# GLA and HGRN over blocks of 512 tokens with all states before all outputs, and dense groups of 24 matmuls that are not broken

## The chip, the cores and the metric

The kernel runs on one core of one Trainium2 chip. The metric is the device time of one execution in microseconds (us); the time before is the median of three runs, 3616.11 us (3611.39 to 3624.22).

The engines are named as in the profile: PE is TensorE's matmuls and PEld its weight loads, DVE is VectorE, ACT ScalarE, POOL GpSimd, SP SyncE, which issues the DMAs.

## What is computed

A decoder of two layers (`DEPTH`), each with four recurrent mixers side by side and a cross attention, for one prompt of 2048 tokens and for eight samples of eight tokens that start from stored states. All four mixers read one projection of the normalized input and write into one output projection:

```python
proj = h @ P['w_in'][l]
p_ret, p_hgrn, p_gla, p_rwkv = jnp.split(proj, ...)
# ret, HGRN, GLA: a gated linear recurrence per token and head
S_t = diag(exp g_t) S_{t-1} + k_t v_t^T ;  o_t = S_t^T q_t
# RWKV-7
S_t = S_{t-1} diag(w_t) - (S_{t-1} kk_t)(kk_t*a_t)^T + v_t k_t^T ;  o_t = S_t r_t
out = jnp.concatenate([o_ret, o_hgrn, o_gla, o_rwkv], axis=-1) @ P['w_out'][l]
x = x + out
x = x + cross_attend(rmsnorm(x, P['norm_x'][l]), ...)
```

HGRN and ret have four heads of 64 keys, GLA four heads of 32 keys, all with 64 values per head. In ret the decay g is one constant per head, in GLA and HGRN it differs from token to token and key to key. The outputs are normalized per head and multiplied by a silu gate.

## The kernel before

**Blocks.** The prompt is worked off in four blocks of 512 tokens (`TB`, NB = 4) in either layer. `block()` emits one block: RWKV's projections and RWKV itself, then GLA's projections and GLA, HGRN's, ret's, the gates and the output projection. Within a block each mixer runs in two halves of 256 tokens (`Seg(False)`, nt = 2 tiles of 128 tokens). Block 0 of a layer also makes the samples' projections, and the sample mixers are put into block 0 (RWKV, GLA) and block 1 (HGRN, ret) by the table `TURN`.

**Dense and small products.** The projections are dense: a panel of 128 output columns takes 24 matmuls of 128x128 weights (three products of high and low parts for each of 8 slices of the input), into the PSUM pool `psd`. The recurrences are small products, of 32 to 128 rows. RWKV, ret and the samples take their PSUM tiles from `psa` and `psc` in turn (lane "ac"), GLA and HGRN from `psb` (lane "b").

**Who sets the order.** The order of each engine is fixed when the program is built, by a list scheduler that takes the ready instruction of highest priority, so that dense matmuls fall into the waits of the small chains. `held()` (lines 212 to 217) decides where a run of matmuls may be broken: every `run[0]`-th matmul of a run has its own priority, and the others are raised by `HOLD` so that they follow at once. `run[0]` is `DENSE` = 12 for a panel of the projections, `SMALL` = 48 for the small products; the output projection sets a run of 12 of its own accord with `DENSE` as well.

**GLA and HGRN.** `dyadic()` computes the scores within a tile of 128 tokens in seven levels s = 1, 2, 4 to 64 (`LEVELS`): at each level a set of 64x32 products (`psb<-dn_hq,dn_hf`), a masked copy into the scores `sT` on DVE (line 736), then the decays are multiplied into q and k (`q_step`, `k_step`; DVE) and into the running totals `tot` (POOL). In GLA two heads of 32 keys share 64 rows; `apart()` makes two masked copies of q by multiplying it with `hm32` on DVE. `outputs()` then goes from tile to tile: it reads the state S for tile t, adds the scores times v, and updates S before tile t + 1. `head_norm()` normalizes `osb`, the outputs; ret's `osb` lies in the tile of `rqT`.

**Memory.** RWKV, ret and the samples' mixers have scratch pools that begin at the lower end of SBUF's free part (`left`: wk1, wk1s, wk4 and others), GLA and HGRN at the upper end (`right`: wk2, wk3). A pool's tiles wait one by one for the earlier tiles that lay at the same place. `wrp` holds three buffers (tag "w") for raw weights, which are staged in block 0 only; the later blocks load weights that are already split.

Of the kernel before, what the change touches and what calls it, by code (L numbers as in the profile page):

```python
# [43 lines left out]
DENSE = 12  # L44
# [89 lines left out]
def decoder(ctx, tc, I, C, O):  # L134
# [428 lines left out]
    class Seg:  # L563
        def __init__(self, sample):
            self.sample = sample
            self.P = SN if sample else 128
            self.nt = 1 if sample else 2
            self.n = self.P * self.nt
            self.levels = SLEVELS if sample else LEVELS
# [26 lines left out]
    def outputs(seg, sT, at, v, qd, S, NG, NC, kT, tot, wp, eps, center, evac, state_out=None):  # L596


        P, nt = seg.P, seg.nt
        KD = 128 // NG  # L600
        NP = NG // 2
        if not seg.sample:
            po = PS("r").rearrange("p (t n) -> p t n", t=2)
            p5 = po.rearrange("p t (c g j d) -> p t c g j d", c=NC, g=2, j=NP)
            es = [slice(0, 64), slice(64, 128)]
            for t in range(nt):
                for c in range(NC):
                    for j in range(NP):
                        for e in es:
                            mm(p5[e, t, c, :, j, :], qd[:, c, j, t * 128 + e.start:t * 128 + e.stop], S[:, c, :], True, False)  # L610
                        for g in range(2):
                            h = c * NG + g * NP + j
                            x = sT[:, at(t, h)].rearrange("p e n -> p (e n)")
                            for e in es:
                                mm(po[e, t, h * 64:(h + 1) * 64], x[:, e], v[:, t, h * 64:(h + 1) * 64], False, True)
                pu = PS("r")[:, :NC * 64].rearrange("p (c n) -> p c n", c=NC)
                for h in range(NH):
                    c, g = divmod(h, NG)
                    mm(pu[g * KD:(g + 1) * KD, c, :], kT[:, t, h * KD:(h + 1) * KD], v[:, t, h * 64:(h + 1) * 64])
                for c in range(NC):  # L620
                    for p in range(2):
                        gs = slice(64 * p, 64 * p + 64)
                        blk = S[gs, c, p * 64:(p + 1) * 64]
                        V.scalar_tensor_tensor(blk, blk, tot(t, c)[gs], pu[gs, c, :], ALU.mult, ALU.add)
            tags = ("rqT", "rkT", None) if center else ("qx2", "qx2", 2)
            o = wp.tile([128, 2, 256], F32, name="osb", tag=tags[0], bufs=tags[2])
            A.activation(o, po, AF.Copy)
            head_norm(o, 128, 2, eps, center, wp, tags[1:], evac)
            return
        bm = sample_const("bmask", wp)  # L630
        pa = PS("r")
# [27 lines left out]
    def place(NG, NC, nt):  # L659

        NP = NG // 2

        def at(t, h):
            c, g = divmod(h, NG)
            p, j = divmod(g, NP)
            return ((p * nt + t) * NC + c) * NP + j
        return at

    def dyadic(seg, q, k, a, NG, NC, sT, wp):
# [10 lines left out]
        mine = lambda x, p: x[:, p * w:(p + 1) * w]  # L680

        def apart(i):
            if NP == 1:
                return q.unsqueeze(2)
# [6 lines left out]
        def products(s, f):  # L691
# [10 lines left out]
            for p in range(2):  # L702
                yield (mine(sT[:P], p)[:, :, 0, :].rearrange("p u (b f s) -> p u b f s", f=2, s=s)[:, :, :, f, :],
# [7 lines left out]
        def q_step(s, tot, x):  # L711
# [5 lines left out]
            new = wp.tile([128, NC, n // (2 * s)], F32, name=f"tot{s}", tag=f"tot{s}")  # L717
# [9 lines left out]
        tt(V, q, q, a, ALU.mult)  # L727
        tot = q_step(1, a, q.unsqueeze(2))
        Q[0] = apart(1)
        for li, s in enumerate(seg.levels):  # L730
# [6 lines left out]
            else:  # L737
                A.activation(sT[64:128, :, 1, :], sT[64:128, :, 0, :], AF.Copy)
                G.memset(sT[64:128, :, 0, :], 0.0)
                ps = [PS("r")[:, :NC * NP * 64].rearrange("p (c g n) -> p c g n", c=NC, g=NP) for _ in range(2)]  # L740
                for c in range(NC):
                    for t in range(nt):
                        for p in range(2):
                            mm(ps[p][64 * t:64 * t + 64, c], k[rows[p], c, t * P:t * P + 64], Q[0][rows[p], c, :, t * P + 64:t * P + 128])
                for t in range(nt):
                    for p in range(2):
                        o = mine(sT[0:64], p)[:, t * NC * NP:(t + 1) * NC * NP, 1, :]
                        A.activation(o, ps[p][64 * t:64 * t + 64].rearrange("p c g n -> p (c g) n"), AF.Copy)
# [4 lines left out]
        return Q[0], tot  # L753
# [18 lines left out]
    def gain(on, col):  # L772
        def f(ps):
            A.activation(on, ps, AF.Copy, scale=col)
        return f

    def plain(on):
        def f(ps):
            A.activation(on, ps, AF.Copy)
        return f  # L780

    def R_gla(l, seg, st, d, on, wp):
        c = cols[l]
        n = seg.n
        qk, v, sm = d["qk"], d["v"], d["sm"]
# [12 lines left out]
        sT = wp.tile([128, seg.nt * NH, seg.P // 64, 64], F32, name="sT", tag="sT")  # L798
        qd, tot = dyadic(seg, qk[:, 0:1, :], qk[:, 1:2, :], a, 4, 1, sT, wp)
        at = place(4, 1, seg.nt)  # L800
        kT = totok(qk[:, 1:2, :], 1, seg, wp, "gmn", 128)
        if seg.sample:
# [4 lines left out]
            outputs(seg, sT, at, v, qk[:, 0:1, :], S, 4, 1, kT, decay, wp, 32 * RMS_EPS, False,  # L807
                    gain(on, c["gla_norm"][:, 0:1]), lambda: sample_state_out(S, O[7][l], 32))
        else:
            outputs(seg, sT, at, v, qd, st, 4, 1, kT, lambda t, cc: tot[:, cc, t:t + 1], wp, 32 * RMS_EPS, False,  # L810
                    gain(on, c["gla_norm"][:, 0:1]))

    def R_hgrn(l, seg, st, d, on, wp):
# [8 lines left out]
        sT = wp.tile([128, seg.nt * NH, seg.P // 64, 64], F32, name="sT", tag="sT")  # L822
        qd, tot = dyadic(seg, q, f, a, 2, 2, sT, wp)
        at = place(2, 2, seg.nt)
        kT = totok(f, 2, seg, wp, "ha", 256)
        if seg.sample:
# [4 lines left out]
            outputs(seg, sT, at, v, q, S, 2, 2, kT, decay, wp, 4 * RMS_EPS, False,  # L831
                    gain(on, c["hgrn_norm"][:, 0:1]), lambda: sample_state_out(S, O[5][l], 64))
        else:
            outputs(seg, sT, at, v, qd, st, 2, 2, kT, lambda t, cc: tot[:, cc, t:t + 1], wp, 4 * RMS_EPS, False,
                    gain(on, c["hgrn_norm"][:, 0:1]))

    def R_ret(l, seg, st, d, on, wp):
# [23 lines left out]
        at = lambda t, h: t * NH + h  # L861
# [12 lines left out]
        if seg.sample:  # L874
# [397 lines left out]
    def block(l, b, act, hts, st, smp, on, ons, ds, op):  # L1272
# [4 lines left out]
        pr, sa = Seg(False), Seg(True)  # L1277
        carry = st["carry"]
# [102 lines left out]
        for hb in range(2):  # L1381
            with within("wk2", hb, 2), on_lane("b"), right("wk2") as wp:
                R_gla(l, pr, st["gla"], dict(qk=h2(qk, hb), v=t2(gv, hb), sm=sm[:, hb * 256:(hb + 1) * 256]), h2(on["gla"], hb), wp)
        if smp:
            ds["gla"] = dict(qk=qks, v=gvs, sm=sms)
# [38 lines left out]
        for hb in range(2):  # L1424
            with within("wk3", hb, 2), on_lane("b"), right("wk3") as wp:
                R_hgrn(l, pr, st["hgrn"], dict(q=h2(hq, hb), f=h2(hf, hb), v=t2(hv, hb)), h2(on["hgrn"], hb), wp)
# [595 lines left out]
```

## Time and profile before

| what | value |
|---|---|
| median of 3 runs | 3616.11 us |
| the profiled execution's own time | 3606.43 us |
| its span | 3604.6 us |
| mean granted clock of TensorE | 0.968 |
| PE busy | 3366.3 us, 93% |
| PEld busy | 2835.7 us, 79% |
| DVE busy | 2112.9 us, 59% |
| ACT busy | 1274.3 us, 35% |
| POOL busy | 553.0 us, 15% |

Busy time of PE is a sum of modelled lengths of pipelined matmuls, so a busy PE may still be short of its peak; that is why starts are compared below, from one row to the next, and not lengths. A clock of 1.00 stands for 2.4 GHz; the other level is 1.2 GHz. An "idle before" in brackets names the engine and the tile that came last before the instruction could start.

### The profile page before, as it was taken

What the parts mean: (1) busy time and instruction counts of PE and PEld (TensorE: products, weight loads), DVE (VectorE), ACT (ScalarE), POOL (GpSimd) and SP (SyncE); (2) the same over time, 40 slices, a digit from 0 to 9 for tenths busy, and PEclk for the clock granted to TensorE, in tenths of its full rate; (3) what the DMA queues carried; (4) which work ended last, traced back from release to release, by engine and by line L of the source; (5) the groups of instructions that cost most, each with busy time, mean ns of one, the idle gap of its engine ahead of it and who ended that gap; (6) DMA issues with size and microseconds to landing.
All of it is one profiled execution on the core that took longest, in us unless ns stands there. A gap on an engine that the chain in (4) does not pass through costs nothing.

```text
span 3604.6 us, 85661 instructions
## 1 busy us (share of the span) xinstructions
PE 3366.3 (93%) x36138; PEld 2835.7 (79%) x36138; DVE 2112.9 (59%) x6047; ACT 1274.3 (35%) x2729; POOL 553.0 (15%) x680
## 2 busy tenths in 40 slices
PE   7998799998999999999999997999889999999998
PEld 5877688886978888888877866878678888878887
DVE  5677545675436754576446765467644567446754
ACT  4442334422243324332344332443213333244323
POOL 3323231020000100011122242111100011000100
PEclk9999899998999999999999997999989999999999
DMA  6522565235662254324453255542445522542255
GB/s 191 184 98 89 180 218 192 77 112 163 200 215 90 82 196 150 135 76 173 170 172 121 83 155 175 197 153 94 136 153 186 176 98 92 188 160 103 76 195 188
DMA packets 241957, 530.79 MB, mean 147 GB/s; under 512 B 66854, under 2 KB 179750, under 8 KB 197542
## 3 DMA queue, kind: packets, MB, share of 16 engines
q1 hardware_dynamic: 241574, 525.31, 42.5%
q8 instruction: 285, 4.67, 0.5%
q14 instruction: 98, 0.80, 0.1%
HBM read 410.10 MB, written 115.16 MB: 146 GB/s over the span
## 4 chain that ended last, share of the span: by engine, by line
PE 75%; DVE 12%; ACT 5%; issue 3%; DMA 3%; POOL 2%; SPq 0%; POOLq 0%; ACTq 0%; DVEq 0%
PE psd L221 39%; PE psc L221 13%; PE psa L221 11%; PE psb L221 6%; PE psa L263 2%; PE psb L263 2%; PE psc L263 2%; DVE rsq L227 1%; DMA wraw<-in_w_in 1%; POOL whl L227 1%; DVE osb L227 1%; DVE hri L283 1%; DVE hss L552 1%; DVE dn_hq L227 0%; DMA whl<-w_low 0%
## 5 line engine op out<-in xcount | busy, mean ns | idle before, releaser
L221 PE MATMUL psd<-act,whl 128*128 128x512 f32 (+1 forms) x4032 | 1008.5, 402 | 28.6 <-DVE th L1266 12.8
L221 PEld LDWEIGHTS psd<-act,whl 128*128 128x128 f32 (+1 forms) x4032 | 741.4, 189 | 203.5 <-DVE th L1266 15.3
L221 PE MATMUL psd<-whl,act 128*128 128x256 f32 x3840 | 541.4, 292 | 7.0 <-POOL whl L227 3.3
L221 PEld LDWEIGHTS psd<-whl,act 128*128 128x128 f32 x3840 | 482.9, 193 | 28.6 <-issue 9.2
L227 POOL TENSOR_TENSOR whl<-wraw,whl 128x1024 fp32r<-128x1024 f32 (+1 forms) x90 | 218.0, 2428 | 383.3 <-ACT whl L349 366.2
L271 POOL TENSOR_TENSOR ri<-ri,mhalf 128x1 f32<-128x1 f32 (+1 forms) x87 | 50.6, 582 | 1103.9 <-DVE ri L270 1065.3
L221 PE MATMUL psd<-whl,oh 128*128 128x256 f32 x1152 | 211.4, 284 | 0.0
L221 PEld LDWEIGHTS psd<-whl,oh 128*128 128x128 f32 x1152 | 177.4, 189 | 0.9 <-issue 0.3
L221 PE MATMUL psd<-whl,ol 128*128 128x256 f32 x576 | 162.8, 283 | 0.0
L349 ACT ACTIVATE whl<-wraw 128x1024 fp32r<-128x1024 f32 (+1 forms) x90 | 94.0, 1048 | 120.9 <-DMA wraw<-in_w_in 40.5
L932 ACT ACTIVATE Xb<-X 32x256 f32<-32x256 f32 (+1 forms) x164 | 67.6, 412 | 166.0 <-DVE X L951 119.9
L221 PEld LDWEIGHTS psd<-whl,ol 128*128 128x128 f32 x576 | 108.5, 188 | 1.0 <-DVE ol L227 1.0
L736 DVE COPY_PREDICATED sT<-upack,psb 128x128 f32<-128x128 uint8 x320 | 89.6, 327 | 33.2 <-PE psb L221 31.5
L227 DVE TENSOR_TENSOR x<-x,psd 128x256 f32<-128x256 f32 x72 | 30.3, 421 | 132.1 <-PE psd L221 132.1
L221 PEld LDWEIGHTS psb<-dn_hq,dn_hf 64*64 64x64 f32 x3840 | 73.9, 135 | 29.5 <-issue 13.9
L221 PE MATMUL psb<-dn_hq,dn_hf 64*64 64x32 f32 (+1 forms) x3840 | 89.2, 223 | 8.0 <-DVE dn_hf L821 3.0
L1266 DVE SCALAR_TENSOR_TENSOR th<-th,psd 128x512 f32<-128x512 f32 x48 | 32.3, 686 | 109.1 <-ACT th L1265 109.1
L426 ACT ACTIVATE xs<-xn 128x1024 f32<-128x1024 f32 (+1 forms) x34 | 35.8, 1053 | 165.8 <-PE psb L263 153.2
L221 PEld LDWEIGHTS psd<-hts,wraw 128*64 128x64 f32 x1984 | 68.8, 144 | 18.9 <-issue 9.6
L221 PE MATMUL psa<-whl,oh 128*128 128x256 f32 x448 | 82.7, 282 | 0.0
L221 PE MATMUL psc<-whl,oh 128*128 128x256 f32 x448 | 82.6, 282 | 0.0
L221 PE MATMUL psd<-hts,wraw 128*64 128x64 f32 x1984 | 78.8, 232 | 3.8 <-DVE th L1266 3.8
(760 smaller groups left out, 6972.5 us busy)
## 6 DMA issues: line engine op xcount, KB each, us to landing
whl<-w_w_out SPq DMA_DIRECT2D x56, 1024.0 KB
wraw<-in_w_in SPq DMA_DIRECT2D x76, 512.0 KB
wraw<-in_w_out SPq DMA_DIRECT2D x32, 512.0 KB
w_w_out<-whl SPq DMA_DIRECT2D x16, 1024.0 KB
x<-x SPq DMA_DIRECT2D x32, 512.0 KB
whl<-w_rw_r SPq DMA_DIRECT2D x12, 1024.0 KB
whl<-w_rw_k SPq DMA_DIRECT2D x12, 1024.0 KB
whl<-w_rw_v SPq DMA_DIRECT2D x12, 1024.0 KB
```

The lines of the kernel that those rows point to most:

```text
L221: PE.matmul(out, lhsT=lhsT, rhs=rhs, start=start, stop=stop, skip_group_check=True)
L227: e.tensor_tensor(out, a, b, op)
L263: PE.transpose(out, in_, ident[:rows, :rows])
L271: G.tensor_tensor(y, y, mhalf[:P], ALU.pow)
L283: V.scalar_tensor_tensor(y, t, 1.5, y, ALU.add, ALU.mult)
L349: A.activation(hl[:, 0], raw, AF.Copy)
L426: A.activation(out, xt, AF.Square, accum_out=ss[:P])
L552: V.tensor_reduce(ss[:P, :n4], sq[:P, :n4], AX.X, ALU.add)
L736: V.copy_predicated(out, bc(mk, [P, w, 32 // s, s]), ps)
L932: A.activation(dst(b), src(b), AF.Copy)
L1266: V.scalar_tensor_tensor(th, th, 1.0, x, ALU.add, ALU.mult)
```

## The change

1. `DENSE` goes from 12 to 24, so that no panel's group of 24 matmuls is broken any more.
2. GLA and HGRN run once per block of 512 tokens (nt = 4) in blocks 1 to 3. Block 0 keeps two halves of 256.
3. `outputs()` first makes all state updates of its nt tiles into one PSUM tile, moves the state from tile to tile into a new tile `Sx`, and then makes all outputs, two tiles of 128 tokens to a PSUM tile. This holds for ret too (nt = 2).
4. `dyadic()` keeps the scores in two tiles instead of one; in blocks 1 to 3 these and `Sx` lie in buffers of `wrp`. The totals take turns in two tags. GLA's q is written twice, masked, when it leaves PSUM (ACT), and `apart()`'s multiplies on DVE are gone for the prompt. GLA's k takes one of the two buffers of the tag "th".

The number of matmuls stays (25,192 in the program before, 25,186 after); DVE has 5,633 instructions instead of 6,049, ACT 2,438 instead of 2,512, POOL 645 instead of 685, SP 855 as before.

```diff
-DENSE = 12
+DENSE = 24
...
-    def outputs(seg, sT, at, v, qd, S, NG, NC, kT, tot, wp, eps, center, evac, state_out=None):
+    def outputs(seg, score, v, qd, S, NG, NC, kT, tot, wp, eps, center, evac, state_out=None):
...
+            if nt > 2:
+                x = wrp.tile([128, nt - 1, NC, 128], F32, name="Sx", tag="w")
+            else:
+                x = wp.tile([128, nt - 1, NC, 128], F32, name="Sx", tag="Sx")
+            G.memset(x, 0.0)
+            St = [S] + [x[:, t] for t in range(nt - 1)] + [S]
+            pu = PS("r")[:, :nt * NC * 64].rearrange("p (t c n) -> p t c n", t=nt, c=NC)
             for t in range(nt):
...
                 for h in range(NH):
                     c, g = divmod(h, NG)
-                    mm(pu[g * KD:(g + 1) * KD, c, :], kT[:, t, h * KD:(h + 1) * KD], v[:, t, h * 64:(h + 1) * 64])
+                    mm(pu[g * KD:(g + 1) * KD, t, c, :], kT[:, t, h * KD:(h + 1) * KD], v[:, t, h * 64:(h + 1) * 64])
...
+            for t in range(nt - 1):
+                move(t)
+            pos = []
+            for t0 in range(0, nt, 2):
+                po = PS("r").rearrange("p (t n) -> p t n", t=2)
...
+                                mm(p5[e, t - t0, c, :, j, :], qd[:, c, j, t * 128 + e.start:t * 128 + e.stop], St[t][:, c, :], True, False)
...
+                pos.append(po)
+            move(nt - 1)
...
+        if nt > 2:
+            sT = [wrp.tile([128, w, nh, 64], F32, name="sT", tag="w") for p in range(2)]
+        else:
+            sT = [wp.tile([128, w, nh, 64], F32, name="sT", tag=f"sT{p}") for p in range(2)]
...
-            if NP == 1:
-                return q.unsqueeze(2)
+            if NP == 1 or not seg.sample:
+                return q if len(q.shape) == 4 else q.unsqueeze(2)
...
-            new = wp.tile([128, NC, n // (2 * s)], F32, name=f"tot{s}", tag=f"tot{s}")
+            size, turn = max(n // (2 * s), 1), (len(bin(s)) + 1) % 2
+            new = wp.tile([128, NC, n // 2 >> turn], F32, name=f"tot{s}", tag=f"tot{turn}")[:, :, :size]
...
+        parts = [slice(0, TB)] if not smp else [slice(0, TB // 2), slice(TB // 2, TB)]
+        gr = Seg(False, NT // len(parts))
...
+        gq = op.tile([128, 1, 2, TB], F32, name="dn_gq", tag="on_hgrn")
+        gk = dnp.tile([128, 1, TB], F32, name="dn_gk", tag="th", bufs=2)
...
+            for j in range(2):
+                A.activation(gq[:, 0, j, :], ps, AF.Copy, scale=K["hm32"][:, j:j + 1])
...
-        for hb in range(2):
-            with within("wk3", hb, 2), on_lane("b"), right("wk3") as wp:
-                R_hgrn(l, pr, st["hgrn"], dict(q=h2(hq, hb), f=h2(hf, hb), v=t2(hv, hb)), h2(on["hgrn"], hb), wp)
+        for x in parts:
+            with within("wk3"), on_lane("b"), right("wk3") as wp:
+                R_hgrn(l, gr, st["hgrn"], dict(q=hq[:, :, x], f=hf[:, :, x], v=hv[:, tiles(x)]), on["hgrn"][:, :, x], wp)
```

Three places of the program show how instructions move. The names: `psd` are dense products, `psb<-dn_hq,dn_hf` HGRN's levels, `Wb`, `Xb` and `X` steps of RWKV, `rqT`, `sT`, `S_ret` and `osb` belong to ret.

PE, first layer, block 2, where HGRN's levels run beside RWKV, before:

```order
L263 MATMUL psc<-fpack,X 128x128 x2
L221 MATMUL psa<-Xb,XB 32x128 x8
L221 MATMUL psb<-dn_hq,dn_hf 64x32 x16
L221 MATMUL psd<-whl,act 128x256 x12
L221 MATMUL psc<-Wb,XB 32x128 x8
L221 MATMUL psb<-dn_hq,dn_hf 64x32 x16
L263 MATMUL psa<-fpack,X 128x128 x2
L221 MATMUL psd<-whl,act 128x256 x12
L221 MATMUL psc<-Xb,XB 32x128 x8
L221 MATMUL psb<-dn_hq,dn_hf 64x32 x16
```

and after:

```order
L221 MATMUL psb<-dn_hq,dn_hf 64x32 x32
L221 MATMUL psd<-whl,act 128x256 x24
L221 MATMUL psa<-fpack,wt_12621 64x2 x8
L221 MATMUL psd<-whl,act 128x256 x24
L221 MATMUL psb<-dn_hq,dn_hf 64x32 x32
L221 MATMUL psd<-whl,act 128x256 x24
L263 MATMUL psc<-fpack,wosb 128x128 x4
L221 MATMUL psc<-sm,w_340 128x256 x2
L221 MATMUL psb<-dn_hq,dn_hf 64x32 x32
```

A dense run of 12 that stood at each step of the chains is one of 24 now, and a level of HGRN has 32 products where it had 16.

PE, the end of the same block, down to the gates (the run of 96), before:

```order
L221 MATMUL psb<-dn_hv,sT 64x64 x4
L221 MATMUL psb<-S_hgrn,dn_hq 64x128 x2
L221 MATMUL psb<-dn_hv,sT 64x64 x4
L221 MATMUL psc<-S_ret,rqT 64x128 x2
L221 MATMUL psc<-dn_rv,sT 64x64 x4
L221 MATMUL psc<-S_ret,rqT 64x128 x2
L221 MATMUL psc<-dn_rv,sT 64x64 x4
L221 MATMUL psd<-act,whl 128x512 x36
L263 MATMUL psb<-fpack,osb 128x128 x4
L221 MATMUL psd<-act,whl 128x512 x12
L263 MATMUL psa<-fpack,osb 128x128 x4
L221 MATMUL psd<-act,whl 128x512 x96
```

and after:

```order
L221 MATMUL psc<-S_ret,rqT 64x128 x2
L221 MATMUL psc<-dn_rv,sT 64x64 x4
L221 MATMUL psc<-S_ret,rqT 64x128 x2
L221 MATMUL psc<-dn_rv,sT 64x64 x4
L221 MATMUL psc<-Sx,rqT 64x128 x2
L221 MATMUL psc<-dn_rv,sT 64x64 x4
L221 MATMUL psc<-Sx,rqT 64x128 x2
L221 MATMUL psc<-dn_rv,sT 64x64 x4
L263 MATMUL psa<-fpack,osb 128x128 x4
L221 MATMUL psd<-act,whl 128x512 x96
```

Two dense runs, of 36 and 12, stood among ret's last products; now none stands there, and the last one ahead of the run of 96 is a run of 24 that ended 112 rows earlier, among RWKV's steps.

DVE, first layer, block 0, the start of HGRN (`ha<-dn_hf`), before:

```order
L227 TENSOR_TENSOR rsq<-rsq,hri 128x8
L283 SCALAR_TENSOR_TENSOR hri<-rsq,hri 128x8
L227 TENSOR_TENSOR osb<-osb,hri 128x512
L930 COPY Wb<-psc 32x8x32 x2
L819 TENSOR_SCALAR ha<-dn_hf,c_129,c_134 128x256 x2
L821 TENSOR_SCALAR dn_hf<-dn_hf,mc_131,c_129 128x256 x2
L951 COPY_PREDICATED X<-upack,psa 128x256
L930 COPY Xb<-X 32x8x32 x2
```

and after:

```order
L227 TENSOR_TENSOR rsq<-hri,rsq 64x4
L227 TENSOR_TENSOR rsq<-rsq,hri 64x4
L283 SCALAR_TENSOR_TENSOR hri<-rsq,hri 64x4
L227 TENSOR_TENSOR wosb<-wosb,hri 64x256
L227 TENSOR_TENSOR qx_3389<-ds_qk,fpack 128x128
L838 TENSOR_SCALAR ha<-dn_hf,c_129,c_134 128x256 x2
L813 TENSOR_SCALAR gmn<-psa,cols_101 128x64
L227 TENSOR_TENSOR sT<-psc,fpack 64x64
L227 TENSOR_TENSOR sT<-psa,fpack 64x64
L840 TENSOR_SCALAR dn_hf<-dn_hf,mc_131,c_129 128x256 x2
```

HGRN's first instruction stood behind the normalization of GLA's outputs (`osb`, 128 rows); now it stands behind that of the sample's RWKV (`wosb`, 64 rows), 136 rows further down.

## Rows read from the trace of the kernel before

**Rows 1.** Page, part 1 (busy time) and part 4 (chain that ended last).
```profile
PE 3366.3 (93%) x36138; PEld 2835.7 (79%) x36138; DVE 2112.9 (59%) x6047; ACT 1274.3 (35%) x2729; POOL 553.0 (15%) x680
PE 75%; DVE 12%; ACT 5%; issue 3%; DMA 3%; POOL 2%; SPq 0%; POOLq 0%; ACTq 0%; DVEq 0%
```

**Rows 2.** Windows by block: stretch, length, busy PE, PEld, DVE, ACT, POOL; PEclk, DMA.
```profile
0.00:466.00 466.00, 399.60 (x4671) 326.98 (x4672) 289.97 (x819) 174.62 (x347) 146.70 (x136) 0.95 0.45 149
...
899.00:1319.00 420.00, 413.87 (x4428) 349.43 (x4427) 233.59 (x693) 140.79 (x310) 32.20 (x60) 1.00 0.45 155
...
1708.00:2224.00 516.00, 466.23 (x5122) 387.40 (x5121) 301.34 (x830) 190.11 (x400) 124.80 (x112) 0.93 0.42 140
...
sum 3604.00, PE 3366.32 PEld 2835.71 DVE 2112.94 ACT 1274.28 POOL 553.00; mean PE 374.04 PEld 315.08 DVE 234.77 ACT 141.59 POOL 61.44
```

**Rows 3.** Windows of five ends of blocks, then two from the middle.
```profile
417.00:448.00 31.00, 15.26 (x113) 12.65 (x111) 19.22 (x52) 8.10 (x14) 7.01 (x5) 0.68 0.52 158
850.00:882.00 32.00, 16.78 (x144) 14.22 (x142) 20.41 (x57) 7.76 (x13) 2.15 (x3) 0.57 0.26 91
2140.00:2207.00 67.00, 44.39 (x339) 34.43 (x338) 38.75 (x106) 14.79 (x25) 15.20 (x11) 0.74 0.38 122
2590.00:2651.00 61.00, 37.79 (x320) 28.89 (x321) 32.40 (x98) 11.34 (x21) 6.22 (x8) 0.66 0.25 77
3068.00:3086.00 18.00, 9.88 (x92) 7.89 (x91) 12.68 (x37) 6.82 (x13) 0.55 (x1) 0.81 0.41 151
1240.00:1302.00 62.00, 58.96 (x770) 50.42 (x767) 47.29 (x163) 19.05 (x35) 6.70 (x13) 1.00 0.29 102
1630.00:1691.00 61.00, 58.73 (x646) 49.19 (x645) 39.34 (x128) 14.85 (x28) 5.66 (x11) 1.00 0.41 143
```

**Rows 4.** Timeline of PE, covered half of ret: start, length, instruction, idle before.
```profile
1242.60 0.66 PE L263 MATMUL psc<-fpack,dn_rq 128*128 128x128 f32 x4
...
1251.14 1.67 PE L221 MATMUL psd<-whl,act 128*128 128x256 f32 x12
1252.74 0.67 PE L221 MATMUL psb<-dn_hq,dn_hf 64*64 64x32 f32 x32
1253.34 1.16 PE L221 MATMUL psa<-rqT,rkT 64*128 64x128 f32 x8
...
1256.86 0.86 PE L221 MATMUL psd<-whl,act 128*128 128x256 f32 x5
1257.65 0.45 PE L221 MATMUL psc<-dn_rv,sT 128*64 128x64 f32 x8
...
1258.72 1.09 PE L221 MATMUL psd<-whl,act 128*128 128x256 f32 x7
1259.74 0.67 PE L221 MATMUL psb<-dn_hq,dn_hf 64*64 64x32 f32 x32
...
1261.06 0.40 PE L221 MATMUL psc<-dn_rv,sT 128*64 128x64 f32 x8
1261.39 0.96 PE L221 MATMUL psd<-act,whl 128*128 128x512 f32 x3
```

**Rows 5.** Timeline of PE, bare half of ret in block 0.
```profile
426.69 1.09 PE L263 MATMUL psa<-fpack,osb 128*128 128x128 f32 x4 [0.73 <-DVE osb L227]
...
445.04 1.09 PE L263 MATMUL psa<-fpack,osb 128*128 128x128 f32 x4 [6.83 <-DVE osb L227]
```

**Rows 6.** Waits of PE: for what, us in total, times, longest us.
```profile
PE psc L263 <- DVE osb L227: 30.0, 7, 6.8
...
PE psa L263 <- DVE osb L227: 22.9, 8, 6.8
PE psd L221 <- DVE th L1266: 16.6, 12, 1.9
```

**Rows 7.** Groups by line (ns min/median/max): the multiplies by hm32, the zeroing of scores.
```profile
L227 DVE TENSOR_TENSOR qx<-dn_qk,fpack x32: 668/692/694, 131.8 to 3313.1; 128x512 f32<-128x512 f32 x32
...
L739 POOL MEMSET sT<- x32: 519/520/584, 163.7 to 3437.1; 64x512 f32 x32
```

More of the change, by code (lines that the diff above doesn't have):

```diff
@@ L622, in outputs @@
                         gs = slice(64 * p, 64 * p + 64)
-                        blk = S[gs, c, p * 64:(p + 1) * 64]
-                        V.scalar_tensor_tensor(blk, blk, tot(t, c)[gs], pu[gs, c, :], ALU.mult, ALU.add)
+                        a, b = (y[gs, c, p * 64:(p + 1) * 64] for y in St[t:t + 2])
+                        V.scalar_tensor_tensor(b, a, tot(t, c)[gs], pu[gs, t, c, :], ALU.mult, ALU.add)
+            for t in range(nt - 1):
[3 more added lines that the diff above has]
+                po = PS("r").rearrange("p (t n) -> p t n", t=2)
+                p5 = po.rearrange("p t (c g j d) -> p t c g j d", c=NC, g=2, j=NP)
+                for t in range(t0, t0 + 2):
+                    for c in range(NC):
+                        for j in range(NP):
+                            for e in es:
+                                mm(p5[e, t - t0, c, :, j, :], qd[:, c, j, t * 128 + e.start:t * 128 + e.stop], St[t][:, c, :], True, False)
+                            for g in range(2):
+                                h = c * NG + g * NP + j
+                                x = score(t, h)
+                                for e in es:
+                                    mm(po[e, t - t0, h * 64:(h + 1) * 64], x[:, e], v[:, t, h * 64:(h + 1) * 64], False, True)
+                pos.append(po)
+            move(nt - 1)
             tags = ("rqT", "rkT", None) if center else ("qx2", "qx2", 2)
-            o = wp.tile([128, 2, 256], F32, name="osb", tag=tags[0], bufs=tags[2])
-            A.activation(o, po, AF.Copy)
-            head_norm(o, 128, 2, eps, center, wp, tags[1:], evac)
+            for t0, po in zip(range(0, nt, 2), pos):
+                o = wp.tile([128, 2, 256], F32, name="osb", tag=tags[0], bufs=tags[2])
+                A.activation(o, po, AF.Copy)
+                head_norm(o, 128, 2, eps, center, wp, tags[1:], lambda ps: evac(ps, t0 * 128))
             return
@@ L737, in dyadic @@
             else:
[L738 to L740 removed]
+                n2 = nt // 2
+                ps = [PS("r")[:, :n2 * NC * NP * 64].rearrange("p (t c g n) -> p t c g n", t=n2, c=NC, g=NP) for _ in range(2)]
+                for p in range(2):
+                    A.activation(sT[p][64:128, :, 1, :], sT[p][64:128, :, 0, :], AF.Copy)
+                    G.memset(sT[p][64:128, :, 0, :], 0.0)
                 for c in range(NC):
@@ L772, in gain, with f @@
     def gain(on, col):
-        def f(ps):
-            A.activation(on, ps, AF.Copy, scale=col)
+        def f(ps, o=0):
+            A.activation(on[:, :, o:o + ps.shape[2]], ps, AF.Copy, scale=col)
         return f
     def plain(on):
-        def f(ps):
-            A.activation(on, ps, AF.Copy)
+        def f(ps, o=0):
+            A.activation(on[:, :, o:o + ps.shape[2]], ps, AF.Copy)
         return f
@@ L784, in R_gla @@
         n = seg.n
-        qk, v, sm = d["qk"], d["v"], d["sm"]
+        q, k, v, sm = d["q"], d["k"], d["v"], d["sm"]
         ps = PS("r")
@@ L797, in R_gla @@
         a = az.unsqueeze(1)
[L798 to L801, printed above, removed]
+        score, qd, tot = dyadic(seg, q, k, a, 4, 1, wp)
+        kT = totok(k, 1, seg, wp, "gmn", 128)
         if seg.sample:
@@ L1380, in block @@
             proj_t("gla_v", lambda ps, t0: copy_ps(gv[:, t0:t0 + 2, :], ps), gvs)
-        for hb in range(2):
-            with within("wk2", hb, 2), on_lane("b"), right("wk2") as wp:
-                R_gla(l, pr, st["gla"], dict(qk=h2(qk, hb), v=t2(gv, hb), sm=sm[:, hb * 256:(hb + 1) * 256]), h2(on["gla"], hb), wp)
+        tiles = lambda x: slice(x.start // 128, x.stop // 128)
+        for x in parts:
+            with within("wk2"), on_lane("b"), right("wk2") as wp:
+                R_gla(l, gr, st["gla"], dict(q=gq[:, :, :, x], k=gk[:, :, x], v=gv[:, tiles(x)], sm=sm[:, x]), on["gla"][:, :, x], wp)
         if smp:
-            ds["gla"] = dict(qk=qks, v=gvs, sm=sms)
+            ds["gla"] = dict(q=qks[:, 0:1, :], k=qks[:, 1:2, :], v=gvs, sm=sms)
         if b == TURN["gla"]:
```

78 lines of the change are left out of this document (32 added, 46 removed).

## The prediction

> **What bounds the kernel now.** The page's busy times and its chain of waits come first: PE is busy for 93% of the span and holds 75% of the chain that ended last, DVE 12% of it [rows 1]. So the time is PE's: its work, its waits and its clock. Next the windows, one for each block of 512 tokens: PE's idle time is a window's length less its busy time. It is 66 us in block 0 of the first layer (466 less 399.6), 6 in block 2 and 50 in block 0 of the second layer, 238 over the nine windows [rows 2]. Then the windows of the ends of blocks, beside two stretches of equal kind in the middle of a block. In the five ends PE is busy for 124 of 209 us and its granted clock lies between 0.57 and 0.81; in the two stretches in the middle it is busy for 117.7 of 123 us at 1.00 [rows 3]. The difference is whether dense matmuls (the projections, psd) stand in PE's order between the products of the recurrences. Where they do, a wait for DVE is filled; at the ends of blocks they have run out, and I call these stretches bare.
>
> What such cover is worth is read from one half (256 tokens) of ret. In a covered half the 14 PE rows that belong to ret (the first is dn_rq's transposes, the last the sT product at 1261.06) take 5.8 us from start to start, 0.2 to 1.1 each, and osb's transposes 0.4 more, 6.2 in all; dense runs and HGRN's products fill the time between them [rows 4]. The bare half in block 0 lasts from the transposes of one osb to those of the next, 426.69 to 445.04, 18.4 us, 6.83 of it in a single wait for the normalization on DVE [rows 5]. So a bare half loses 18.4 less 6.2, 12.2 us. Ret's two halves can't overlap, since osb lies in rqT's tile, and ret can't begin before RWKV's second half is done with the same memory.
>
> **The change part by part.** (1) Panels of 24 unbroken. PE's order holds 633 runs of dense matmuls before and 409 after, 224 fewer. What a run costs beside its matmuls: runs of 5, 7 and 12 take 0.79, 1.02 and 1.60 us from their start to the next row's [rows 4], a line of 0.116 us for each matmul and 0.21 us for the run. 224 times 0.21 is 47 us, the one end; the other is half of it, 24, since a run that goes leaves two small products of unlike shape side by side, whose meeting costs too. I take 36, between the two: -36 us.
>
> (2) The same 24 take cover away from the ends. The scheduler sets a piece of dense work wherever a chain of small products waits. Before, a wait got 12 matmuls (1.60 us); now it gets 24 (about 3.0), whether it is long or short. RWKV's and ret's chains have as many steps as before, so the block's dense work is used up sooner. The order shows it: in block 2 two dense runs stood between ret's last products and the final transposes; now none stands in the 112 rows from RWKV's last steps to the gates. By the order, ret's halves stand bare twice in seven blocks and once in the eighth, 15 in all. Before, it was about 6; PE's waits for osb on the lanes of RWKV and ret add up to 52.9 us in 15 waits, and at 6.8 for each bare half they can't be more than 8 [rows 6]. Nine more at 12.2 us: +110 us. Ends: nine times 8, if DVE, with less to do, answers faster (+72), and nine times 15, if the ends of RWKV's normalization stand bare too (+135).
>
> (3) In block 0 of either layer HGRN moves. Its scratch has grown and now overlaps that of the sample's RWKV by 32 bytes, so its first instruction on DVE stands behind that sample's last normalization instead of right behind GLA. Its two halves thus come when the dense work is gone. A half of HGRN is eight sets of products of 0.60 us [rows 4] with outputs and transposes, some 8 us of PE; with the rest of the sample's RWKV I estimate 30 us of small products that become bare in each of these blocks. At the rate of the bare windows (209 us for 124 busy, and half of that time at the lower clock), 30 become some 70, a loss of 40; but these blocks already waited for 50 and 27 us outside their ends [rows 2, 3], and half of the loss is in there. +20 for each block, +40 us; ends 0 and +80.
>
> (4) What long runs gain in the middle of blocks. Of PE's 238 us of idle time 85 are in the bare windows, 153 are not. A piece of 3.0 us hides a wait that a piece of 1.6 left open. GLA and HGRN by 512 tokens have half as many dependent steps in blocks 1 to 3, each over twice the columns, and DVE loses 416 of its 6,049 instructions: 32 multiplies by hm32 of 0.69 us alone make 22 us [rows 7], for which ACT gets 16 more copies of about 0.6 us. DVE is busy for 59%, so this counts only through PE's waits. I take a little under half of the 153: -70 us; ends -20 (the waits sit where no dense work is left) and -130.
>
> (5) At nothing: the zeroing of Sx on POOL (15% busy, 0.52 us for a zeroing of scores [rows 7]); the staging buffers that now hold scores in blocks 1 to 3, in which no raw weights are staged; k in one of the two buffers of th. If this last cover goes, a projection of silu waits for k to be transposed, 1.9 us at most for each, as PE's longest wait for th [rows 6]; ends 0 and +10. No DMA is added or moved on SP.
>
> The sum: -36 + 110 + 40 - 70 = **+44 us** on the profiled execution's 3606.4, 3650. The median of the runs, 3616.1, lies 9.7 above that execution; on its scale the forecast is **3660 us**, and its own range 3630 to 3700.
>
> **Clock.** The rows show 1.00 where cover stands and 0.57 to 0.81 in the bare windows [rows 3], so there PE spends part of the time at 1.2 instead of 2.4 GHz after its waits of 5 to 7 us. The Trainium skill (TensorE: Matmul & The Clock Gate, HAM oscillation — how this bites in real kernels) says that a kernel whose matmuls come in bursts between waits runs each burst at the lower clock. By that rule alone every one of the new bare stretches would run at the lower clock throughout, which makes the third rival; the trace agrees with it in part, 0.57 in one end and 0.81 in another.
>
> **The rivals.** *Faster, 3570 us.* The middle of blocks gives much more than a half: 110 of the 153, and the bare halves cost 10 instead of 12.2, HGRN nothing: -36 - 110 + 90 + 10 = -46. For it: each block loses time in its middle beyond idle PE, since block 0 keeps the weight loads busy for 327 of 466 us and block 2 for 349 of 420 [rows 2], and dependent steps are halved there. Against it: the middle windows are already at 118 of 123. With the sum's bare terms it decides from a gain of 114 in the middle on (110 + 40 - 36). [...]
>
> *No change, 3616 us.* Bare ends at their lower end of 72, HGRN at 20, the middle at -56, and the 36 cancel.
>
> *Much slower, 3750 us.* All bare time at the lower clock, and nothing gained in the middle, because DVE's long chains over 512 columns make PE wait for longer at once: -36 + 120 + 80 - 30 = +134. For it: 0.57 in the end of block 1 [rows 3]. Against: DVE has less to do.
>
> That the change doesn't do what it says is excluded by the order: the runs of 12 are gone in the projections.
>
> **The numbers.** Chances: the forecast 0.46, faster 0.30, no change 0.11, much slower 0.13. 0.3% is about what a measurement of this kernel can tell from no change. Faster by more than that 0.30, within it 0.11, slower 0.59. The range, 3545 to 3735, leaves out the worse part of the much slower case and the best of the faster one.
>
> **What would show it.** In the profile after, each block should end in 18 to 19 us for each half of ret, with waits for osb of 5 to 7 us, some 15 of them, and a clock under 0.8; DVE's first ha in block 0 should come behind the sample's last osb; blocks 2 and 6 should grow the most against before (by some 25 to 30 us), blocks 1 and 5 hardly; idle time in the middle of blocks should shrink. If blocks 2 and 6 are no longer than before, step (2) is wrong; if block 0 shrinks, step (3).

## The result and the profile after

The changed kernel takes **3788.18 us** (median of 4 runs, 3782.12 to 3795.23) against 3615.78 us before: a ratio of 1.048, 95% interval 1.0465 to 1.0495. It is 172 us slower; 3660 was forecast, with a range up to 3735. The profiled execution spans 3786.8 us against 3604.6, 182 us more.

The page of the changed kernel, part 1, busy time by engine (it answers to [rows 1]):

```profile
PE 3397.2 (90%) x36126; PEld 2885.2 (76%) x36126; DVE 2062.2 (54%) x5631; ACT 1256.6 (33%) x2655; POOL 539.8 (14%) x640
```

The windows of the changed kernel, one for each block, cut at the same point of the program as [rows 2]; the columns are those of [rows 2]:

```profile
0.00:505.00 505.00, 419.63 (x4659) 344.46 (x4660) 284.18 (x809) 175.52 (x350) 145.56 (x145) 0.86 0.42 136
505.00:953.00 448.00, 405.42 (x4382) 344.35 (x4381) 252.20 (x701) 148.29 (x310) 69.67 (x75) 0.92 0.44 147
953.00:1396.00 443.00, 412.35 (x4437) 352.22 (x4437) 228.29 (x630) 138.69 (x298) 29.73 (x51) 0.96 0.41 145
1396.00:1782.00 386.00, 367.75 (x3995) 318.38 (x3994) 223.20 (x606) 129.82 (x277) 33.32 (x56) 0.99 0.41 142
1782.00:2324.00 542.00, 479.51 (x5100) 400.31 (x5099) 297.67 (x814) 189.79 (x401) 124.08 (x120) 0.86 0.39 130
2324.00:2793.00 469.00, 415.06 (x4400) 349.65 (x4399) 260.82 (x716) 155.18 (x324) 70.19 (x79) 0.91 0.43 142
2793.00:3257.00 464.00, 423.12 (x4456) 360.61 (x4455) 241.56 (x645) 145.51 (x313) 33.30 (x56) 0.94 0.40 140
3257.00:3673.00 416.00, 378.53 (x3991) 327.10 (x3990) 228.77 (x612) 134.78 (x287) 29.53 (x50) 0.95 0.35 125
```

The blocks of the kernel before that [rows 2] leaves out:

```profile
466.00:899.00 433.00, 403.52 (x4370) 339.60 (x4369) 261.13 (x763) 150.07 (x322) 70.42 (x84) 0.96 0.45 151
...
1319.00:1708.00 389.00, 378.33 (x4000) 322.67 (x4000) 231.16 (x674) 133.80 (x291) 34.53 (x66) 1.00 0.38 136
...
2224.00:2668.00 444.00, 410.81 (x4387) 345.16 (x4386) 265.65 (x778) 156.72 (x336) 72.45 (x88) 0.95 0.45 148
2668.00:3101.00 433.00, 418.24 (x4453) 351.95 (x4452) 248.46 (x714) 150.61 (x328) 35.35 (x66) 0.99 0.43 150
3101.00:3493.00 392.00, 380.88 (x4001) 324.81 (x4000) 235.22 (x679) 137.44 (x300) 32.17 (x60) 0.99 0.37 132
```

Against before the eight blocks are longer by 39, 15, 23, -3, 26, 25, 31 and 24 us. No block gains but the fourth, and the granted clock falls in all eight.

Where it is lost is seen at the ends. These are the windows of the stretches at the end of each block in which no dense matmul stands, in the changed kernel. Before, the five of [rows 3] were 209 us long with 124 us of PE:

```profile
363.00:487.00 124.00, 89.94 (x1133) 65.52 (x1132) 75.83 (x249) 27.66 (x62) 24.67 (x43) 0.58 0.18 51
866.00:937.00 71.00, 39.67 (x336) 29.07 (x335) 36.31 (x106) 11.67 (x24) 10.98 (x15) 0.60 0.24 68
1319.00:1379.00 60.00, 35.21 (x524) 31.40 (x523) 36.43 (x110) 15.80 (x29) 5.72 (x9) 0.74 0.15 51
1747.00:1766.00 19.00, 9.86 (x116) 8.27 (x114) 14.10 (x41) 6.52 (x12) 2.42 (x6) 0.82 0.39 131
2164.00:2306.00 142.00, 98.61 (x1172) 71.71 (x1171) 86.70 (x294) 32.40 (x79) 26.61 (x44) 0.55 0.15 42
2687.00:2776.00 89.00, 51.54 (x435) 35.35 (x435) 43.71 (x139) 12.75 (x26) 12.22 (x17) 0.57 0.18 50
3178.00:3239.00 61.00, 34.95 (x519) 30.91 (x517) 34.84 (x106) 13.64 (x26) 4.71 (x8) 0.72 0.09 31
3605.00:3655.00 50.00, 26.38 (x321) 22.82 (x319) 30.03 (x92) 9.00 (x16) 4.16 (x7) 0.66 0.09 28
sum 616.00, PE 386.16 PEld 295.04 DVE 357.96 ACT 129.43 POOL 91.49; mean PE 48.27 PEld 36.88 DVE 44.74 ACT 16.18 POOL 11.44
```

Bare stretches grew from 209 to 616 us, and PE's idle time in them from 85 to 230. All of PE's idle time grew from 238 to 390 (3787 less 3397.2), so outside these stretches it is 160 where it was 153. The 182 us by PE's account are 145 of idle time at bare ends, 7 elsewhere, and 31 more of busy time. The busy time grew in spite of 224 fewer dense runs, at a clock of 0.921 instead of 0.968.

The waits of PE that answer to [rows 6], in the changed kernel:

```profile
PE psc L263 <- DVE osb L227: 47.2, 9, 6.9
PE psa L263 <- DVE osb L227: 41.4, 8, 6.9
PE psa L263 <- DVE wosb L227: 17.8, 7, 6.5
```

Ret's waits for its normalization went from 52.9 to 88.6 us, and RWKV's (`wosb`), of which `psa` had 1.5 us before, came to 17.8. The timeline of PE in block 2, the two halves of ret from one normalization to the next, against the covered half of [rows 4]:

```profile
1342.56 1.09 PE L263 MATMUL psa<-fpack,wosb 128*128 128x128 f32 x4 [5.98 <-DVE wosb L227]
...
1359.08 1.09 PE L263 MATMUL psc<-fpack,osb 128*128 128x128 f32 x4 [6.36 <-DVE osb L227]
...
1375.77 1.08 PE L263 MATMUL psa<-fpack,osb 128*128 128x128 f32 x4 [6.90 <-DVE osb L227]
```

The halves take 16.5 and 16.7 us; covered, a half takes 6.2 of PE. And this is where the dense work went. PE's timeline of the changed kernel, block 1, a step of RWKV's solver (from one transposition of `X` to the next):

```profile
683.40 0.44 PE L263 MATMUL psa<-fpack,X 128*128 128x128 f32 x2
684.35 0.64 PE L221 MATMUL psc<-Xb,XB 128*32 128x128 f32 x16 [0.51 <-ACT Xb L949]
684.92 5.73 PE L221 MATMUL psd<-act,whl 128*128 128x512 f32 x24
690.59 0.65 PE L221 MATMUL psa<-Wb,XB 128*32 128x128 f32 x16
...
691.80 0.44 PE L263 MATMUL psc<-fpack,X 128*128 128x128 f32 x2
```

When `Wb` was ready is read from DVE's timeline of the same stretch:

```profile
686.58 0.43 DVE L947 COPY Wb<-psc 32x256 f32<-32x256 f32 x1 [0.44 <-ACT Wb L949]
```

A step of the kernel before with the same dense work, block 2 of the first layer (PE's rows, then DVE's last copy of `Wb`):

```profile
1118.23 0.38 PE L263 MATMUL psa<-fpack,X 128*128 128x128 f32 x2
...
1119.50 3.02 PE L221 MATMUL psd<-act,whl 128*128 128x512 f32 x12
1122.45 0.65 PE L221 MATMUL psa<-Wb,XB 128*32 128x128 f32 x16
...
1123.41 3.04 PE L221 MATMUL psd<-act,whl 128*128 128x512 f32 x12
1126.29 0.38 PE L263 MATMUL psc<-fpack,X 128*128 128x128 f32 x2
```

```profile
1120.69 0.43 DVE L930 COPY Wb<-psc 32x256 f32<-32x256 f32 x1
```

Both steps hold 24 dense matmuls of 512 columns and are nearly equally long, 8.4 and 8.1 us. The difference is where the dense work can stop. With runs of 12 each of two waits gets 3.0 us, and `Wb`, ready at 1121.12, is read at 1122.45, 1.3 us later. With a whole panel one wait gets 5.7 us, and `Wb`, ready at 687.01, is read at 690.59, 3.6 us later. PE isn't idle, so nothing looks wrong there; but dense work that fills more than the wait delays the chain and is missing at the end.

RWKV's solver has 136 products in each profile that read a copy `Wb` or `Xb`. From the end of the last copy to the start of its product there pass 128 us in sum before and 223 in the changed kernel; dense matmuls run for 97 and 205 of them.

### The profile page after: what moved, and what is told of

It is laid out like the page before. It is cut to its first block, busy times and chain, and to the rows that moved or that the text cites. A ratio compares the mean times of both kernels' runs of the same rounds, so it can differ in the third digit from the quotient of the medians.

```text
span 3786.8 us, 85124 instructions
## 1 busy us (share of the span) xinstructions
PE 3397.2 (90%) x36126; PEld 2885.2 (76%) x36126; DVE 2062.2 (54%) x5631; ACT 1256.6 (33%) x2655; POOL 539.8 (14%) x640
## 5 line engine op out<-in xcount | busy, mean ns | idle before, releaser
L221 PE MATMUL psd<-act,whl 128*128 128x512 f32 (+1 forms) x4032 | 983.8, 400 | 21.1 <-DVE th L1283 9.0
L221 PEld LDWEIGHTS psd<-act,whl 128*128 128x128 f32 (+1 forms) x4032 | 752.4, 189 | 200.2 <-issue 14.3
L221 PE MATMUL psd<-whl,act 128*128 128x256 f32 x3840 | 516.9, 291 | 11.6 <-POOL whl L227 8.3
L227 POOL TENSOR_TENSOR tot<-tot 128x8 f32<-128x8 f32 (+7 forms) x128 | 38.1, 298 | 456.8 <-DVE dn_gq L227 231.6
L755 DVE COPY_PREDICATED sT<-upack,psb 128x256 f32<-128x256 uint8 (+1 forms) x200 | 77.2, 427 | 23.6 <-PE psb L221 22.1
```

Source lines behind the costliest of these rows:

```text
L221: PE.matmul(out, lhsT=lhsT, rhs=rhs, start=start, stop=stop, skip_group_check=True)
L227: e.tensor_tensor(out, a, b, op)
L755: V.copy_predicated(out, bc(mk, [P, w, 32 // s, s]), ps)
```

## The experiments

**1. Runs of 12 in the changed kernel.**

```diff
-DENSE = 24
+DENSE = 12
```

> The change with runs of 12 again, all else kept. Theory (cover): the loss comes from unbroken groups of 24, which use up the dense work before a block's end. Then the bare ends shrink from 616 us to about what they were before (180) or a little more, since the order of this kernel leaves bare ends only in block 0 of both layers and block 1 of the second; time 3580 to 3660, PE idle back under 260 us. Rival (the new form of GLA and HGRN, blocks of 512 tokens and states first, makes the loss): the time stays above 3720 and the idle time near 380.

Measured: 3646.03 us, ratio 1.0084 (1.0067 to 1.0101). The unbroken groups are most of the loss: 142 of the 172 us go with this one number, and RWKV's delays behind ready copies fall from 223 to 88 us. PE's idle time, 281 us, stays above the 260 that were expected. Windows of blocks 0 of the two layers:

```profile
0.00:492.00 492.00, 412.58 (x4658) 338.31 (x4659) 293.91 (x809) 174.92 (x350) 146.96 (x145) 0.90 0.43 139
1726.00:2260.00 534.00, 477.08 (x5107) 395.30 (x5106) 295.50 (x820) 190.84 (x403) 123.99 (x121) 0.88 0.40 133
```

They are still 26 and 18 us longer than before, 44 together, so they hold all of the 32 us that remain by the medians.

**2. Groups of 24 in the kernel before.**

```diff
-DENSE = 12
+DENSE = 24
```

> The kernel before with groups of 24 and nothing else of the change. Theory (cover): slower than the change itself, because halves of 256 tokens have twice as many dependent steps, each of which now takes a whole panel; small products that stand bare are 400 us by the medians of before's rows against 364 in the change and 190 before, so 3616 + 172*(210/174), about 3820. Rival (the new form of GLA and HGRN makes the loss): 36 us faster than before for 217 fewer dense runs, about 3580.

Measured: 3908.25 us, ratio 1.0815 (1.0798 to 1.0832). The number alone costs 294 us, more than the whole change; what else the change does gave 120 back. The order and the sign were as the theory had them, the size was underestimated by 88 us. The eight blocks end here in 785 us without dense work, where the change has 616 and the kernel before 209, and RWKV's delays behind ready copies are 321 us.

**3. Two halves of 256 in every block, groups of 24.**

```diff
-        parts = [slice(0, TB)] if not smp else [slice(0, TB // 2), slice(TB // 2, TB)]
+        parts = [slice(0, TB // 2), slice(TB // 2, TB)]
```

> The change with two halves of 256 tokens in every block; groups of 24, states first, masked q kept. Theory (cover): slower than the change, 3800 to 3860, with small bare products of 412 us by the medians against 364; blocks of 512 tokens are then a gain of the change, not its loss. Rival (long chains over 512 tokens make PE wait): faster than the change, under 3740, with the gain in blocks 1 to 3.

Measured: 3854.7 us, ratio 1.0661 (1.0642 to 1.068). With groups of 24, blocks of 512 tokens gain 66 us. The reading that fits is half as many waits, each of which would eat a panel; experiments 11 and 12 try it with shorter runs. The remaining 54 us to the kernel of experiment 2 belong to the rest of the change.

**4. HGRN early in block 0.** `Sx` shares the slot of `osb`, so that the scratch no longer overlaps.

```diff
-                x = wp.tile([128, nt - 1, NC, 128], F32, name="Sx", tag="Sx")
+                x = wp.tile([128, nt - 1, NC, 128], F32, name="Sx", tag="Sx" if center else "qx2", bufs=None if center else 2)
```

> The change with the new tile Sx of GLA and HGRN in block 0 laid into a slot that already exists, so that HGRN's scratch no longer overlaps that of the sample's RWKV and HGRN can start right behind GLA. Theory (cover): with groups of 24 the dense work is gone all the same, the bare small products fall only from 364 to 347 us, so 10 to 20 us less, 3768 to 3778. Rival (HGRN's late start is what blocks 0 lose, 39 and 26 us): 3720 to 3735.

Measured: 3770.42 us, ratio 1.0433 (1.0415 to 1.0452), 18 us less than the change. HGRN's first instruction on DVE starts at 285 us instead of 394 in the first layer, so the edit does what it is meant to. HGRN's place costs that much with groups of 24; that the rest of what blocks 0 lose is the groups' is argued, not shown here.

**5. HGRN early and runs of 12**: the edits of experiments 1 and 4 together.

```diff
-DENSE = 24
+DENSE = 12
...
-                x = wp.tile([128, nt - 1, NC, 128], F32, name="Sx", tag="Sx")
+                x = wp.tile([128, nt - 1, NC, 128], F32, name="Sx", tag="Sx" if center else "qx2", bufs=None if center else 2)
```

> The change with runs of 12 and with HGRN's scratch in block 0 clear of the sample's RWKV, as in the run before this one that did so. Theory (cover): the 32 us that runs of 12 left over against the kernel before lie in blocks 0 of the two layers (26 and 19 us longer there by the profiles, the other blocks 3 us shorter in sum), where HGRN comes late; with HGRN early they go, and what is left of the change is worth a little: 3590 to 3615. Rival (states before outputs, or the masked copies of q, cost those 32 us): no better than 3635.

Measured: 3613.83 us, ratio 0.9991 (0.998 to 1.0001). The 32 us are gone, and with them the excess of block 0:

```profile
0.00:466.00 466.00, 392.72 (x4670) 324.80 (x4671) 299.92 (x814) 175.74 (x352) 146.68 (x146) 0.95 0.47 149
1705.00:2227.00 522.00, 466.92 (x5119) 387.49 (x5118) 309.72 (x825) 191.77 (x405) 126.84 (x122) 0.92 0.42 138
```

Block 0 takes 466 us, as before; the fifth takes 522, still 6 more. HGRN's first instruction starts at 263 us, where experiment 1 had it at 371. So HGRN's late start, which the prediction puts down to 32 bytes of overlap between two scratch pools, costs 32 us here.

**6. HGRN early and runs of 6**: the same kernel with another length.

```diff
-DENSE = 12
+DENSE = 6
```

> The same with runs of 6. Theory (cover): finer pieces keep more dense work for the ends; small products that stand bare fall from 173 us (runs of 12) to 130 by before's medians, at the price of 99 more dense runs at 0.16 us, 16 us; with the exchange rate of the runs so far (about 1.0 to 1.3 us of time for 1 us of bare products) 25 to 40 us faster than runs of 12. Rival (switching between dense and small products costs more than cover is worth): 15 us or more slower than runs of 12.

Measured: 3530.79 us, ratio 0.9758 (0.9744 to 0.9772). It is 83 us faster than with runs of 12, twice what was expected. PE's waits for ret's normalization, then the longest stretch without a dense matmul:

```profile
PE psc L263 <- DVE osb L227: 15.4, 5, 6.9
...
PE psa L263 <- DVE osb L227: 9.6, 4, 6.3
```

```profile
2558.00:2589.00 31.00, 15.43 (x177) 13.69 (x176) 19.25 (x60) 6.32 (x12) 1.50 (x3) 0.67 0.18 53
```

The waits fell from 52.9 us in the kernel before to 25.0, the longest bare end from 142 us in the change to 31, and RWKV's delays behind ready copies to 57 us, with dense matmuls running for 33 of them.

**7. Runs of 6 in the kernel before.**

```diff
-DENSE = 12
+DENSE = 6
```

> The kernel before with runs of 6 instead of 12. Theory (cover): bare small products fall from 190 to 112 us for 106 more dense runs (17 us): 3535 to 3600. Rival (switching decides): 3632 or more.

Measured: 3589.85 us, ratio 0.9922 (0.9904 to 0.994). Shorter runs help there too, by 26 us.

**8. Added work in the bare ends.** Nobody reads `pw`; the added products keep PE at work in the waits. A few transposes of the next block (`xs`) move behind them in PE's order.

```diff
+    warm = [None]
...
             move(nt - 1)
+            if center:
+                pw = psb.tile([128, 512], F32, name="psb", tag="b")
+                y = warm[0]
+                for i in range(4):
+                    mm(pw, y[:, 7, :], y[:, 4:8, :].rearrange("p a n -> p (a n)"), i == 0, i == 3)
...
         score = lambda t, h: sT[:P, t * NH + h]
+        warm[0] = sT
```

> The change with added work: four products of 128x512 on ret's scores behind the outputs of each half of ret, 64 in all, whose result nobody reads (some 3.5 us of PE for each half at 2.4 GHz, 55 us in sum), to stand in the wait for the normalization. Theory (the lower clock is a good part of what a bare end costs): a bare half of ret, 18 us, loses 2 to 4 us because PE comes back at the full clock, and the kernel gets 20 to 50 us faster although it does more. Rival (only the waits cost): no faster, 0 to 20 us slower.

Measured: 3824.09 us, ratio 1.0572 (1.0552 to 1.0591), 36 us slower than the change and outside both expectations. Windows of the ends of blocks 2 of the two layers:

```profile
1326.00:1386.30 60.30, 41.58 (x540) 33.73 (x538) 35.83 (x110) 15.51 (x29) 5.71 (x9) 0.83 0.15 49
...
3199.60:3261.70 62.10, 41.98 (x535) 34.15 (x533) 34.19 (x106) 13.78 (x26) 4.70 (x8) 0.80 0.09 28
```

The clock rose from 0.74 to 0.83 and from 0.72 to 0.80, and the ends took 60 and 62 us, where they had taken 60 and 61. PE's timeline of the first of them shows the added products and the normalizations around them:

```profile
1350.66 1.09 PE L263 MATMUL psa<-fpack,wosb 128*128 128x128 f32 x4 [6.39 <-DVE wosb L227]
...
1360.12 3.70 PE L221 MATMUL psb<-sT 128*128 128x512 f32 x8
...
1367.13 0.63 PE L263 MATMUL psc<-fpack,osb 128*128 128x128 f32 x4 [2.87 <-DVE osb L227]
...
1383.28 1.09 PE L263 MATMUL psa<-fpack,osb 128*128 128x128 f32 x4 [0.38 <-DVE osb L227]
```

The first half still takes 16.5 us, as it must, since the added products stand behind its own. The second takes 16.2 instead of 16.7. Windows from a half's first transposes to ACT's copy of its outputs, first two of the change (blocks 2 and 3), then the second half here:

```profile
1359.08:1368.93 9.85, 9.11 (x88) 8.35 (x88) 4.44 (x13) 1.20 (x3) 0.00 (x0) 0.53 0.00 1
...
1747.43:1754.46 7.03, 6.28 (x99) 5.45 (x97) 4.83 (x15) 1.19 (x2) 1.55 (x4) 1.00 0.62 224
```

```profile
1367.13:1374.73 7.60, 6.86 (x89) 6.33 (x90) 4.00 (x12) 1.09 (x3) 0.00 (x0) 0.78 0.01 2
```

So the clock does cost something. Behind a wait of 6.4 us ret's products of a half take 9.85 us at a granted clock of 0.53; behind the added products they take 7.60 at 0.78; behind a dense run they take 7.03 at 1.00. Most of the 2.3 us that experiment 8 gains there is lost again in the normalization, which takes 8.55 us (1374.73 to 1383.28) instead of 6.84 (1368.93 to 1375.77). DVE now works on the next block among its rows, behind the transposes of `xs` that have moved:

```profile
1379.13 0.42 DVE L227 TENSOR_TENSOR xg<-psb,cols 128x256 f32<-128x256 f32 x1
...
1381.37 0.75 DVE L430 TENSOR_SCALAR xs<-xn,ri 128x1024 f32<-128x1024 f32 x1 [0.33 <-POOL ri L271]
```

The run thus doesn't decide what a raised clock alone is worth. By the first dense matmul behind each bare end, blocks 0 of the two layers became 12 and 16 us longer and blocks 1 became 6 and 3 us shorter. In blocks 0 the added products stand among other chains, and what lengthens them is not isolated.

**9. HGRN early and runs of 4**: on the kernel of experiment 6.

```diff
-DENSE = 6
+DENSE = 4
```

> As the run with runs of 6 and HGRN early (3531), with runs of 4. Theory (cover, with a price for switches): no further gain, since by before's medians the bare small products are 157 us against 130 and there are 46 more dense runs (7 us): 3540 to 3575. Rival (the finer the better): 3500 to 3520.

Measured: 3525.99 us, ratio 0.9752 (0.9729 to 0.9775), between the two expectations and not to be told from runs of 6. No further gain is seen.

**10. Runs of 6, HGRN late**: the change with one number altered.

```diff
-DENSE = 24
+DENSE = 6
```

> The change with runs of 6 and nothing else, so HGRN's scratch in block 0 overlaps that of the sample's RWKV again. Theory: HGRN's late start in the two blocks 0 costs as with runs of 12 (32 us) or 24 (18 us), by the bare products 26 us: 3550 to 3565, all of it in the first and the fifth block. Rival (with fine runs enough dense work is left to cover a late HGRN): within 8 us of 3531.

Measured: 3567.61 us, ratio 0.9865 (0.9845 to 0.9885), just above the range that was expected. HGRN's late place costs 37 us, even with fine runs.

**11. Runs of 6, HGRN early, two halves in every block**: the edit of experiment 3 on the kernel of experiment 6.

```diff
-        parts = [slice(0, TB)] if not smp else [slice(0, TB // 2), slice(TB // 2, TB)]
+        parts = [slice(0, TB // 2), slice(TB // 2, TB)]
```

> Runs of 6, HGRN early, but two halves of 256 tokens in every block. Theory: the blocks of 512 tokens, which have half as many dependent steps in blocks 1 to 3, are what makes this kernel faster than the one before with runs of 6 (3590): here 3570 to 3595. Rival (states first and the masked copies of q do it): within 15 us of 3531.

Measured: 3535.31 us, ratio 0.9782 (0.9752 to 0.9811). The rival was right: with runs of 6 blocks of 512 tokens are worth nothing (5 us, inside the noise), and the rest of the change is worth 55 us against experiment 7. Of these three lengths, fewer steps helped only with groups of 24 (experiments 3, 11 and 12).

**12. Runs of 12, HGRN early, two halves**: on the kernel of experiment 11.

```diff
-DENSE = 6
+DENSE = 12
```

> Runs of 12, HGRN early, two halves of 256 tokens in every block: the kernel before with states first, masked copies of q and the new tiles, and nothing else of the change. These were worth 54 us with runs of 24 and 55 with runs of 6 (halves against the kernel before, each at the same length of run). Theory (they are worth that much in themselves): 3555 to 3580, and then blocks of 512 tokens cost some 45 us at runs of 12. Rival (what they are worth depends on where the bare ends fall, since this order has a bare stretch of 20 us of small products in either of blocks 4 and 5 where that of before has 14 and 20): 3600 to 3630.

Measured: 3592.06 us, ratio 0.9943 (0.9923 to 0.9962). Neither expectation holds: the rest of the change is worth 21 us here, and blocks of 512 tokens cost some 20 (22 by the medians, 17 by the ratios). Why these two depend on the run's length so is open; orders with runs of 12 differ in where the bare ends fall, but no run isolates that.

All medians together, in us (columns: length of the unbroken runs):

| form | 24 | 12 | 6 | 4 |
|---|---|---|---|---|
| kernel before | 3908 | 3616 | 3590 | |
| change, halves, HGRN late | 3855 | | | |
| change, halves, HGRN early | | 3592 | 3535 | |
| change (512 tokens), HGRN late | 3788 | 3646 | 3568 | |
| change (512 tokens), HGRN early | 3770 | 3614 | 3531 | 3526 |

Each row rises with the length of the run, but 6 and 4 can't be told apart. The change with runs of 6 or 4 and `Sx` moved beats both kernels, 2.4% under the one before.

## Why the prediction was wrong

The sign was right, and so was the mechanism behind the loss: groups of 24 use up the dense work and leave the blocks' ends bare. The time left the range on the side of the third rival, "much slower", 3750.

In the sum's own terms, the bare ends are 407 us longer, and 231 us of PE's busy time left the rest of the span (a busy us counted alike at either clock). That is a loss of 176 us at the ends, for which (2) and (3) had 150. Outside the ends the time fell by 225 us while those 231 us left, so nothing was gained there, where (1) and (4) had 106. Most of the miss of 138 us on the profiled execution is this gain that didn't come.

**(1), -36 us for fewer runs.** Not seen by itself. PE's busy time rose by 31 us instead, while more of it lies in stretches at the lower clock. No run isolates what a run costs: 106 dense runs more, and shorter, made the kernel before 26 us faster (experiment 7), but that is the price and the better cover together.

**(2) and (3), bare ends, +110 and +40.** A bare half of ret was sized well, 16.5 us against 18.4. But the term counted ret's halves only. Block 2's bare end begins at 1319 with RWKV's last steps, 24 us before ret's part of it; 15 halves of 16.5 make 248 of the 616 us, so 368 us stood bare outside them (some 200 of these in blocks 0). That the two terms come near the 176 us is partly luck: HGRN's late start is 18 us (experiment 4), not 40, and the ends of RWKV, which no term counted, stand in for it.

**(4), -70 us for the middle of blocks.** This is the step that failed. "A piece of 3.0 us hides a wait that a piece of 1.6 left open": idle time outside the bare ends went from 153 to 160, beyond the step's own worst end of -20. The step took a longer run to be better cover. A run can't be broken once the chain's next product is ready, so the chain is held up by it, for 223 us instead of 128 in RWKV's solver; and with the panels of 512 columns a run is 5.7 us, not 3.0. The rest of the change, half as many dependent steps among it, did gain 120 us with groups of 24 (experiment 2 against the change). The term had both in one, so the longer runs' own share was not a gain but a loss: 294 us in the kernel before, 142 in the changed one.

**The clock.** The third rival had all bare time at the lower clock, and the windows show nearly that (0.55 to 0.60 in the four longest ends). What it costs in ret's halves can be read from equal products: 9.85 us at 0.53 and 7.03 at 1.00, a difference of 2.8 us in a half of 16.5. For 14 bare halves at the lower level that is some 40 us, an estimate from these two rows; in the prediction this price stands within the 12.2 us of a bare half. What it costs in RWKV's ends is open. The Trainium skill (TensorE: Matmul & The Clock Gate, HAM oscillation — how this bites in real kernels) advises, for matmuls in short bursts between DMA waits, to restructure the loop so that PE stays warm. The waits here are for DVE; where added products kept PE at work the trace agrees (9.85 to 7.60 us), but the kernel with them was 36 us slower.

**What was named as a test.** Some 15 waits for osb, a clock under 0.8, ha behind the sample's RWKV: so it is, with 17 waits of 88.6 us in sum, the longest 6.9, and with one short end of eight at 0.82. Halves of 18 to 19 us: 16.5 to 16.7 in block 2. That blocks 2 and 6 grow by 25 to 30 us: 23 and 31. That blocks 1 and 5 hardly grow: wrong, 15 and 25, as RWKV's bare steps weigh there too. That idle time in the middle shrinks: wrong.

## What to carry to other kernels

Filler work that hides the waits of a dependent chain should come in pieces no longer than the waits: a longer piece shows no idle time where it stands, but it holds up the chain and is missing at the end. Look for the loss where the filler has run out, not where it was lengthened, and count every chain that then stands bare, not only the last. When scratch pools share memory from both ends, look at what a few more bytes make wait for what.

## What the runs showed that was not expected

Added matmuls raised TensorE's granted clock in ret's products from 0.53 to 0.78 and shortened them from 9.85 to 7.60 us, and yet the bare end stayed at 60 us: the same edit let DVE's work for the next block into the normalization, which took 1.7 us longer. And runs of 6 and even of 4 matmuls were faster than runs of 12, by 83 to 88 us in the changed form. By the prediction's estimate of 0.21 us for a dense run [rows 4], 99 more runs (runs of 6) would cost 21 us, so the better cover would be worth some 100.
